# Down stages of a decoder layer: the last hidden pair is used later in the first product, and the row statistics of the later column groups are taken later in the next stage

## The chip, the cores and the metric

The kernel runs on one core of a Trainium2 chip. A core has five engines with instruction streams of their own: TensorE (PE in the profile; its weight loads, which overlap the products, are PEld), VectorE (DVE), ScalarE (ACT), GpSimd (POOL) and SyncE (SP), which here only starts transfers; 16 DMA engines carry them. The metric is the device time of one launch in microseconds (us).

## The reference

One inference step of one layer of a hybrid decoder, for a prompt of 1024 tokens and eight decode requests of one token each, 1032 rows in all. The model width is 1024, the hidden width of each feed-forward network (FFN) is 2816, and everything is float32.

```python
def swiglu(x, wg, wu, wd):
    return (jax.nn.silu(x @ wg) * (x @ wu)) @ wd

    h = x + 0.5 * swiglu(rmsnorm(x, lw['g_ff1']), lw['w_ff1_gate'], lw['w_ff1_up'], lw['w_ff1_down'])
    z = rmsnorm(h, lw['g_mix']) @ lw['w_in']
    ...
    mix = jnp.concatenate([rmsnorm(a, lw['g_attn_out']), hm], axis=-1) @ lw['w_out']
    h = h + mix
    h = h + 0.5 * swiglu(rmsnorm(h, lw['g_ff2']), lw['w_ff2_gate'], lw['w_ff2_up'], lw['w_ff2_down'])
    h = h + jax.nn.sigmoid(rmsnorm(h, lw['g_ple']) @ lw['w_ple_gate']) * (pe @ lw['w_ple_proj'])
```

Between `z` and `mix` stand attention with a low-rank latent cache (`a`) and an mLSTM with matrix memory (`hm`); a last `rmsnorm` follows. What matters here are the two FFNs, the product that stands behind each (`w_in` behind the first, `w_ple_gate` behind the second), and the row norm between them: `rmsnorm(h)` needs the sum of the squares of each row of `h` over all 1024 features.

## The kernel before

**Layout and arithmetic.** Activations lie with features on the 128 partitions and the 1032 tokens along the free axis, so `h` is eight tiles of 128 x 1032 (`KD` = 8, index k). For the projections the tokens are cut into three groups of 344 (`G`, index g), for the FFNs into four quarters of 258. A float32 product is made of three matmuls on rounded parts: high by high, high by low, low by high (`mm3`, L219 to L222). So each operand is first split: ScalarE writes the rounded high part, VectorE subtracts it from the original and writes the low part. Large tiles come from 43 shared SBUF buffers (`B`), short-lived ones of 344 columns from nine scratch buffers (`SC`), accumulators from eight PSUM banks (`PS`).

**An FFN** is one call of `ffn` (L425 to L697). Its first part makes the gate and up products and from them the hidden tiles, 22 of 128 features, in 11 pairs p (`NP`). It also forms the sums of tiles that the seven products of the next part need, and `store` (L461 to L470) writes them to a DRAM tensor `hidd[7, 2, 128, NP, QN]`: for each pair and each half hf of the columns two POOL transfers, `hid<-hp` (L469, products' operands 0 to 3) and `hid<-gs` (L470, operands 4 to 6). The last pair, 10, is stored last.

**The down stage** is a scheme of seven products i (table `DOWN`, L41 to L47) in place of eight. Each has two halves hf, each half walks the 11 pairs, and one step is one pair: twelve matmuls into four accumulators `pd`. That makes 7 x 2 x 11 = 154 steps (`NSTEP`). After the last pair of a half VectorE adds the four accumulators, times plus or minus one half, into two to four places of `h` (L677).

The loads that feed the steps are planned by step number. `at(n, fn)` puts a function on a heap, and `fetch(n)` runs all that are due before the matmuls of step n. `load_w` fetches a double pair of weights and plans its sum and its split 5, 6 and 7 steps later. `load_x` (L596 to L610) fetches the hidden tiles of four pairs from `hidd`, 11 steps before their first use (`X_LEAD`), and plans their high part on ScalarE (L603) 6 steps after the load and the low part on VectorE (L606) 7 steps after it. Its third load of a half holds pairs 8 to 10. `load_h` fetches the eight tiles of `h` from step -3 on, and `aheads` names steps at which weights of the next stage are loaded. Items with negative step numbers, and those up to step 4, are run inside the last chunk of the gate and up part.

All these loads are started by SyncE, which takes its instructions strictly in the written order; one that has to wait for a store blocks the ones behind it. Inside the down stage TensorE, SyncE, VectorE and ScalarE all keep the written order (`DOWN_ENGINES`, L657 to L684). Outside it TensorE and SyncE keep it, and a planner orders the other engines.

**The norm behind an FFN** is an object of class `Rows` (L307 to L337), `nu` before the input projection and `npl` before the last stage. `ops(g, k)` multiplies a tile of `h` by its gain and splits it into the operands of the next product (ScalarE L322, VectorE L323). `square(g, k)` squares it on ScalarE (L327) and adds it on VectorE (L331) to the running sum of the group, which takes a scratch buffer. `scale(g)` calls `norm_r` (L285): a matmul with a matrix of ones (`ns`, L287) sums over the partitions, ScalarE takes the reciprocal root (L291), and VectorE refines it with a Newton step. The result multiplies the product's output, not its input, so a product of group g needs `ops(g, k)` to start, and `scale(g)` before its evacuation; the code asserts that `scale(g)` is written before the unit.

Before the change the last ten steps of a down stage do `ops` of groups 0 and 1, two a step in the order of groups, one `square(0, k)` a step, and then `scale(0)`. `ops(2, k)` stands behind the last step. The sums of groups 1 and 2 belong to the generator `stats` (L686 to L697): for each of the two groups four ticks with two squares each, one empty tick, then `scale(g)`. The emitter (L115 to L152) advances a generator once per so many microseconds of *planned* time, which `em.spend` counts; for `stats` that is 1.2, and one unit of the following product spends 3.5.

**The stages behind.** The input projection (from L1158) runs 22 columns of weights times three groups, 66 units of 24 matmuls (`pz`, L220 to L222). `units(22, EARLY)` (L343) gives their order: the first `EARLY` columns go group by group, the rest column by column with the three groups in a row. So with `EARLY` = 3, group 1 starts at the fourth unit and group 2 at the seventh. `win_unit` (L851) loads weights three columns ahead. After unit (3, 0) the generator `gates` of the mLSTM's gates is started, one tick per 7 planned us; what is left of it is run at unit (9, 2). The last stage (`ple_unit`, L1733) runs eight columns times three groups, group by group, 24 units of 24 matmuls (`pl`); `final(g)` (L1769) is its norm.

Of the kernel before, what the change touches and what calls it, by code (L numbers as in the profile page):

```python
# [23 lines left out]
KD = D // 128  # L24
# [8 lines left out]
NWC = (NP + 1) // 2  # L33
NXC = (NP + 3) // 4
W_ISSUE = (-19, -15, -11, -8, -4, -1)
# [37 lines left out]
LAT_FIN = 12.0  # L73
EARLY = 3
LIFT_POOL = (0, 2, 4)
# [80 lines left out]
def trunk(ctx: ExitStack, tc, I, O):  # L156
# [267 lines left out]

    def ffn(build, X, pre, part, resid, h, nxt, ahead, aheads):  # L425

# [139 lines left out]
        def at(n, fn):  # L566
            heapq.heappush(items, (n, next(count), fn))
# [27 lines left out]

        def load_x(s, i, hf, t):  # L596
            n = min(4, NP - 4 * t)
            raws = [B([128, 4, QN], F32, "hr")]
            sp.dma_start(out=raws[0][:, 0:n], in_=hidd[DOWN[i][1][hf], hf, :, 4 * t:4 * t + n, :])

            def high():
                xh[i, hf, t] = [B([128, 4, QN], F32R, x) for x in ("hh", "hl")]
                act.copy(xh[i, hf, t][0][:, 0:n], raws[0][:, 0:n])  # L603

            def low():
                dve.tensor_tensor(out=xh[i, hf, t][1][:, 0:n], in0=raws[0][:, 0:n], in1=xh[i, hf, t][0][:, 0:n].bitcast(F32), op=ALU.subtract)  # L606
                raws.pop()

            at(s + X_HI, high)
            at(s + X_LO, low)  # L610

# [4 lines left out]
        for i in range(7):  # L616
# [4 lines left out]
            for hf in range(2):  # L621
                for t in range(NXC):
                    s = n + NP * hf + 4 * t - X_LEAD
                    at(s, lambda s=s, i=i, hf=hf, t=t: load_x(s, i, hf, t))
        for m in range(KD):
# [3 lines left out]
        n = NSTEP - NP + 1  # L629
        for g in range(2):  # L630
            for k in range(KD):
                at(n + (KD * g + k) // 2, lambda g=g, k=k: nxt.ops(g, k))
        for k in range(KD):
            at(n + k, lambda k=k: nxt.square(0, k))
        at(n + KD + 1, lambda: nxt.scale(0))

# [20 lines left out]
        ctx2 = ExitStack()  # L657
        ctx2.enter_context(tc.manual_schedule(engines={mybir.EngineType[x] for x in DOWN_ENGINES}))
        for n in range(NSTEP):
            fetch(n)  # L660
            i, hf, p = n // (2 * NP), n // NP % 2, n % NP
            if p == 0:
                acc = [PS([128, QN], "pd") for _ in range(4)]
            (whi, wlo), (xhi, xlo) = wdh[i, p // 2], xh[i, hf, p // 4]
            for m in range(4):
                c = slice(m * 128, (m + 1) * 128)
                mm3(acc[m], whi[:, p % 2, c], wlo[:, p % 2, c], xhi[:, p % 4, :], xlo[:, p % 4, :], p == 0, p == NP - 1)
            whi = wlo = xhi = xlo = None
            if hf == 1 and (p % 2 == 1 or p == NP - 1):
                wdh.pop((i, p // 2))  # L670
            if p % 4 == 3 or p == NP - 1:
                xh.pop((i, hf, p // 4))
            if p == NP - 1:
                for m in range(4):
                    for r, j, sign in DOWN[i][2]:
                        t = h[4 * r + m][:, QS[j if hf == 0 else 3 - j]]
                        dve.scalar_tensor_tensor(out=t, in0=acc[m], scalar=0.5 * sign, in1=t, op0=ALU.mult, op1=ALU.add)  # L677
                acc = None
            em.spend(1.44)
# [6 lines left out]
        def stats():  # L686
            for g in (1, 2):
                for k in range(KD):
                    nxt.square(g, k)
                    if k % 2:  # L690
                        yield
                yield
                nxt.scale(g)
# [120 lines left out]

    ffn(build1, X1, pre1, "1", lambda m: I["xT"][m * 128:(m + 1) * 128, :], h, nu, load_in, AH_IN)
    u = nu.x
# [337 lines left out]
    for n, (i, g) in enumerate(us):  # L1154
        win_unit(i, g)
        if (i, g) == (3, 0):
            em.add(gates_gen, 7.0)
# [570 lines left out]

    ffn(build2, X2, pre2, "2", lambda m: hsp2[m * 128:(m + 1) * 128, :], h, npl, load_p, AH_P)
    xp = npl.x  # L1730
# [174 lines left out]
```

## Time and profile before

| | |
|---|---|
| median of 3 runs | 2246.82 us (2246.46 to 2249.53) |
| the profiled execution's own time | 2244.91 us |
| span of its trace | 2243.1 us |
| busy: TensorE, VectorE, ScalarE, GpSimd | 96%, 65%, 41%, 14% |
| first down stage (first to last `pd`) | starts at 504.98 us |
| input projection | starts at 741.70 us |
| second down stage | starts at 1868.9 us |
| last stage | starts at 2108.8 us |

One execution is profiled; all times are in microseconds from the start of its span. Busy time of TensorE is the modelled time of pipelined matmuls, so 96% doesn't say that it runs at its best pace: at a lower granted clock the same matmul counts for longer. A row of waits names the waiting engine and line, then what it waited for, then the summed wait, how many there were, and the longest. A row of a window names its stretch and length, then for TensorE, its weight loads, VectorE, ScalarE and GpSimd the busy time with the number of instructions in brackets, then the granted clock (1.00 is full), the busy share of the DMA engines and GB/s. A row of the timeline has the start, the duration, the engine, the line and the operation, output before the arrow and inputs behind it.

### The profile page before, as it was taken

The numbers are of one execution on the slowest core, as the hardware profiler recorded it, in microseconds if no ns is written. First come the engines' busy times: TensorE is split into PE (matmuls) and PEld (weight loads), VectorE is DVE, ScalarE is ACT, GpSimd is POOL, SyncE is SP. The second block draws the span as 40 slices with busy tenths as digits, with TensorE's granted clock in tenths as the row PEclk, the third lists the DMA queues.
The fourth block names the chain that finished last, engine by engine and source line by source line (L and its number), as shares of the span: only waits on it lengthen the run. The fifth ranks groups of instructions, "written<-read, shape, count | busy, mean of one in ns | idle before, by whom it ended". The sixth has DMA issues, their size and how long they took to land.

```text
span 2243.1 us, 40124 instructions
## 1 busy us (share of the span) xinstructions
PE 2156.2 (96%) x16225; PEld 2045.1 (91%) x16225; DVE 1457.9 (65%) x2882; ACT 914.1 (41%) x1749; POOL 322.1 (14%) x353
## 2 busy tenths in 40 slices
PE   8999999998999999999999999999999998999787
PEld 7999999998999899999855579999999998999786
DVE  6756656566776647556666777775665655776846
ACT  6333333332343433434455653433333332333633
POOL 2000001000000021111277424100010100000012
PEclk8999999999999999999999999999999999999898
DMA  6122323239875422223555431232232337876213
GB/s 246 53 90 90 123 72 123 90 119 363 271 250 172 157 35 88 87 87 107 165 140 144 152 117 67 84 107 90 81 118 86 109 105 282 317 261 222 81 35 105
DMA packets 106242, 307.80 MB, mean 137 GB/s; under 512 B 14448, under 2 KB 32464, under 8 KB 106056
## 3 DMA queue, kind: packets, MB, share of 16 engines
q1 hardware_dynamic: 82200, 233.75, 31.3%
q0 software_dynamic: 20400, 67.26, 9.3%
q10 hardware_dynamic: 3456, 4.23, 0.7%
q8 instruction: 127, 2.08, 0.4%
q14 instruction: 59, 0.48, 0.1%
HBM read 236.61 MB, written 68.57 MB: 136 GB/s over the span
## 4 chain that ended last, share of the span: by engine, by line
PE 75%; issue 10%; DVE 8%; DMA 3%; ACT 2%; POOL 1%; SPq 0%; DVEq 0%; ACTq 0%; POOLq 0%
PE c L454 9%; PE c L455 9%; PE c L456 9%; PE pd L221 6%; PE pd L222 6%; PE pd L220 6%; PE pz L220 3%; PE pz L222 3%; PE pz L221 3%; PE pss L1482 3%; PE po L1537 2%; PE pT L1514 1%; PE pl L221 1%; PE pl L220 1%; PE pl L222 1%
## 5 line engine op out<-in xcount | busy, mean ns | idle before, releaser
L454 PE MATMUL c<-xh,wh 128*128 128x258 f32 x1920 | 543.3, 283 | 0.9 <-ACT u L532 0.9
L455 PE MATMUL c<-xl,wh 128*128 128x258 f32 x1920 | 542.5, 283 | 0.0
L456 PE MATMUL c<-xh,wl 128*128 128x258 f32 x1920 | 542.5, 283 | 0.0
L454 PEld LDWEIGHTS c<-xh,wh 128*128 128x128 f32 x1920 | 362.6, 189 | 1.5 <-ACT u L532 1.5
L455 PEld LDWEIGHTS c<-xl,wh 128*128 128x128 f32 x1920 | 363.7, 189 | 0.0
L456 PEld LDWEIGHTS c<-xh,wl 128*128 128x128 f32 x1920 | 362.6, 189 | 0.0
L221 PE MATMUL pd<-hl,wh 128*128 128x258 f32 x1232 | 352.0, 286 | 9.7 <-DVE hl L606 9.7
L220 PE MATMUL pd<-hh,wh 128*128 128x258 f32 x1232 | 351.8, 286 | 8.1 <-ACT hh L603 8.1
L222 PE MATMUL pd<-hh,wl 128*128 128x258 f32 x1232 | 350.8, 285 | 0.0
L206 DVE TENSOR_TENSOR wl<-wr,wh 128x1024 fp32r<-128x1024 f32 x166 | 207.4, 1250 | 72.5 <-ACT wh L202 39.4
L221 PEld LDWEIGHTS pd<-hl,wh 128*128 128x128 f32 x1232 | 236.0, 192 | 11.7 <-DVE hl L606 11.4
L220 PEld LDWEIGHTS pd<-hh,wh 128*128 128x128 f32 x1232 | 235.8, 191 | 9.5 <-ACT hh L603 9.1
L222 PEld LDWEIGHTS pd<-hh,wl 128*128 128x128 f32 x1232 | 235.9, 192 | 0.0
L202 ACT CAST wh<-wr 128x1024 fp32r<-128x1024 f32 x166 | 173.0, 1047 | 54.4 <-DVE wr L412 46.2
L585 ACT CAST wh<-wr 128x1024 fp32r<-128x1024 f32 x84 | 81.9, 977 | 253.9 <-issue 141.9
L220 PE MATMUL pz<-u,wh 128*128 128x344 f32 x528 | 172.9, 328 | 0.0
L222 PE MATMUL pz<-u,wl 128*128 128x344 f32 x528 | 169.1, 320 | 0.0
L221 PE MATMUL pz<-u,wh 128*128 128x344 f32 x528 | 168.9, 320 | 0.0
L470 POOL DMA_DIRECT2D hid<-gs x44 | 33.1, 751 | 838.8 <-DVE gs L465 700.5
L588 DVE TENSOR_TENSOR wl<-wr,wh 128x1024 fp32r<-128x1024 f32 x84 | 95.4, 1136 | 73.7 <-ACT wh L585 73.7
L606 DVE TENSOR_TENSOR hl<-hr,hh 128x1032 fp32r<-128x1032 f32 (+1 forms) x84 | 95.6, 1139 | 19.2 <-ACT hh L603 18.6
L220 PEld LDWEIGHTS pz<-u,wh 128*128 128x128 f32 x528 | 99.7, 189 | 0.7 <-issue 0.2
(406 smaller groups left out, 4592.5 us busy)
## 6 DMA issues: line engine op xcount, KB each, us to landing
wr<-in_wd SPq DMA_DIRECT2D x120, 512.0 KB, 5.1
hr<-hid SPq DMA_DIRECT2D x56, 516.0 KB, 5.1
hid<-hp POOLq DMA_DIRECT2D x44, 516.0 KB, 5.5
wr<-in_wg SPq DMA_DIRECT2D x44, 512.0 KB, 4.4
wr<-in_wu SPq DMA_DIRECT2D x44, 512.0 KB, 4.0
hid<-gs POOLq DMA_DIRECT2D x44, 387.0 KB, 4.3
wr<-in_w_in SPq DMA_DIRECT2D x22, 512.0 KB, 4.7
hr<-hid SPq DMA_DIRECT2D x28, 387.0 KB, 5.8
```

The costliest lines, as they stand in the source:

```text
L202: act.copy(hi, src)
L206: dve.tensor_tensor(out=lo, in0=src, in1=hi.bitcast(F32), op=ALU.subtract)
L220: pe.matmul(ps, whi, xhi, start=first, stop=False)
L221: pe.matmul(ps, whi, xlo, start=False, stop=False)
L222: pe.matmul(ps, wlo, xhi, start=False, stop=last)
L454: pe.matmul(ps, whi[:, c], xhi[:, k, :], start=first and k == 0, stop=False, skip_group_check=True)
L455: pe.matmul(ps, whi[:, c], xlo[:, k, :], start=False, stop=False, skip_group_check=True)
L456: pe.matmul(ps, wlo[:, c], xhi[:, k, :], start=False, stop=last and k == 3, skip_group_check=True)
L585: act.copy(wdh[i, c][0][:, 0:n], raws[0][:, 0:n])
L588: dve.tensor_tensor(out=wdh[i, c][1][:, 0:n], in0=raws[0][:, 0:n], in1=wdh[i, c][0][:, 0:n].bitcast(F32), op=ALU.subtract)
L606: dve.tensor_tensor(out=xh[i, hf, t][1][:, 0:n], in0=raws[0][:, 0:n], in1=xh[i, hf, t][0][:, 0:n].bitcast(F32), op=ALU.subtract)
L1482: pe.matmul(ps[:, 0:n], qp[:, qs], kp[0:96, kc], start=True, stop=True)
```

## The change

Six edits:

1. *Order of the first product.* A table `STEPS` gives the steps of each product. In the first product the step of half 0 and pair 10 moves behind the first four steps of half 1, from step 10 to step 14. Since half 0 is then unfinished while half 1 runs, each half has accumulators of its own (`accs`).
2. *Size of the loads.* A table `XC` gives the loads of hidden tiles. In the first product pairs 8 and 9 are one load and pair 10 is another, for both halves; the other six products keep pairs 8 to 10 together.
3. *Lead of the last load.* A load that holds pair 10 alone is planned 8 steps ahead of its use, with its two casts 4 and 5 steps later (`X_LATE`); the others keep 11, 6 and 7.
4. *Last ten steps of a down stage.* `ops(0, k)` go one a step, `square(0, k)` two a step, `ops(1, k)` start four steps later (one a step, then two), and `scale(0)` comes one step earlier.
5. *Statistics of groups 1 and 2.* `ffn` takes a parameter `lag`, the number of empty ticks between the last square of a group and its `scale`: 5 for the first FFN, 14 for the second, in place of 1. For the first FFN `EARLY` goes from 3 to 4, so that group 1 starts at the fifth unit and group 2 at the ninth.
6. *Gates.* The generator `gates` is started after unit (4, 0), not (3, 0).

```diff
-NXC = (NP + 3) // 4
+
+STEPS = [[(hf, p) for hf in range(2) for p in range(NP)] for _ in range(7)]
+STEPS[0] = STEPS[0][0:10] + STEPS[0][11:15] + [(0, 10)] + STEPS[0][15:]
+XC = [((0, 4), (4, 4), (8, 2), (10, 1))] + [((0, 4), (4, 4), (8, 3))] * 6
+X_LATE = (8, 4, 5)
...
-EARLY = 3
+EARLY = 4
...
-        def load_x(s, i, hf, t):
-            n = min(4, NP - 4 * t)
+        def load_x(s, i, hf, t, s_hi, s_lo):
+            p0, n = XC[i][t]
             raws = [B([128, 4, QN], F32, "hr")]
-            sp.dma_start(out=raws[0][:, 0:n], in_=hidd[DOWN[i][1][hf], hf, :, 4 * t:4 * t + n, :])
+            sp.dma_start(out=raws[0][:, 0:n], in_=hidd[DOWN[i][1][hf], hf, :, p0:p0 + n, :])
...
-            at(s + X_HI, high)
-            at(s + X_LO, low)
+            at(s + s_hi, high)
+            at(s + s_lo, low)
...
-                for t in range(NXC):
-                    s = n + NP * hf + 4 * t - X_LEAD
-                    at(s, lambda s=s, i=i, hf=hf, t=t: load_x(s, i, hf, t))
+                for t, (p0, _) in enumerate(XC[i]):
+                    lead = X_LATE if p0 == NP - 1 else (X_LEAD, X_HI, X_LO)
+                    s = n + STEPS[i].index((hf, p0)) - lead[0]
+                    at(s, lambda s=s, i=i, hf=hf, t=t, lead=lead: load_x(s, i, hf, t, *lead[1:]))
...
-        for g in range(2):
-            for k in range(KD):
-                at(n + (KD * g + k) // 2, lambda g=g, k=k: nxt.ops(g, k))
         for k in range(KD):
-            at(n + k, lambda k=k: nxt.square(0, k))
-        at(n + KD + 1, lambda: nxt.scale(0))
+            at(n + k, lambda k=k: nxt.ops(0, k))
+            at(n + 4 + min(k, 4 + (k - 4) // 2), lambda k=k: nxt.ops(1, k))
+            at(n + k // 2, lambda k=k: nxt.square(0, k))
+        at(n + KD, lambda: nxt.scale(0))
...
+        accs = [None, None]
         for n in range(NSTEP):
             fetch(n)
-            i, hf, p = n // (2 * NP), n // NP % 2, n % NP
+            i = n // (2 * NP)
+            hf, p = STEPS[i][n % (2 * NP)]
             if p == 0:
-                acc = [PS([128, QN], "pd") for _ in range(4)]
+                accs[hf] = [PS([128, QN], "pd") for _ in range(4)]
+            acc = accs[hf]
...
-                yield
+                for _ in range(lag):
+                    yield
                 nxt.scale(g)
                 yield
...
-        if (i, g) == (3, 0):
+        if (i, g) == (4, 0):
             em.add(gates_gen, 7.0)
```

The calls of `ffn` pass `lag` as 5 and 14.

More of the change, by code (lines that the diff above doesn't have):

```diff
@@ L423, in weights, with ffn @@
         return work
-    def ffn(build, X, pre, part, resid, h, nxt, ahead, aheads):
+    def ffn(build, X, pre, part, resid, h, nxt, ahead, aheads, lag):
         W = [I["wg" + part], I["wu" + part]]
@@ L658, in ffn @@
         ctx2.enter_context(tc.manual_schedule(engines={mybir.EngineType[x] for x in DOWN_ENGINES}))
+        accs = [None, None]
         for n in range(NSTEP):
             fetch(n)
-            i, hf, p = n // (2 * NP), n // NP % 2, n % NP
+            i = n // (2 * NP)
+            hf, p = STEPS[i][n % (2 * NP)]
             if p == 0:
-                acc = [PS([128, QN], "pd") for _ in range(4)]
-            (whi, wlo), (xhi, xlo) = wdh[i, p // 2], xh[i, hf, p // 4]
+                accs[hf] = [PS([128, QN], "pd") for _ in range(4)]
+            acc = accs[hf]
+            t = next(t for t, (p0, k) in enumerate(XC[i]) if p0 <= p < p0 + k)
+            x = p - XC[i][t][0]
+            last = x == XC[i][t][1] - 1
+            (whi, wlo), (xhi, xlo) = wdh[i, p // 2], xh[i, hf, t]
             for m in range(4):
                 c = slice(m * 128, (m + 1) * 128)
-                mm3(acc[m], whi[:, p % 2, c], wlo[:, p % 2, c], xhi[:, p % 4, :], xlo[:, p % 4, :], p == 0, p == NP - 1)
+                mm3(acc[m], whi[:, p % 2, c], wlo[:, p % 2, c], xhi[:, x, :], xlo[:, x, :], p == 0, p == NP - 1)
             whi = wlo = xhi = xlo = None
@@ L670, in ffn @@
                 wdh.pop((i, p // 2))
-            if p % 4 == 3 or p == NP - 1:
-                xh.pop((i, hf, p // 4))
+            if last:
+                xh.pop((i, hf, t))
             if p == NP - 1:
@@ L677, in ffn @@
                         dve.scalar_tensor_tensor(out=t, in0=acc[m], scalar=0.5 * sign, in1=t, op0=ALU.mult, op1=ALU.add)
-                acc = None
+                acc = accs[hf] = None
             em.spend(1.44)
@@ L813, in load_in @@
         win_w[i] = loadw(I["w_in"][i], KD)
-    ffn(build1, X1, pre1, "1", lambda m: I["xT"][m * 128:(m + 1) * 128, :], h, nu, load_in, AH_IN)
+    ffn(build1, X1, pre1, "1", lambda m: I["xT"][m * 128:(m + 1) * 128, :], h, nu, load_in, AH_IN, 5)
     u = nu.x
@@ L1727, in load_p @@
         wp[j] = loadw(I["w_pg"][j], KD)
-    ffn(build2, X2, pre2, "2", lambda m: hsp2[m * 128:(m + 1) * 128, :], h, npl, load_p, AH_P)
+    ffn(build2, X2, pre2, "2", lambda m: hsp2[m * 128:(m + 1) * 128, :], h, npl, load_p, AH_P, 14)
     xp = npl.x
```

## The prediction

> **What bounds the kernel now.** First the page's head, the engines' shares and the chain that ended last.
>
> ```profile
> span 2243.1 us, 40124 instructions
> PE 75%; issue 10%; DVE 8%; DMA 3%; ACT 2%; POOL 1%; SPq 0%; DVEq 0%; ACTq 0%; POOLq 0%
> ```
>
> TensorE carries three quarters of the chain, so time is to be had only where it stands still or runs slowly. The second view, TensorE's own waits, says where.
>
> ```profile
> PE ns L287 <- DVE sq L331: 25.2, 5, 10.9
> PE pd L221 <- DVE hl L606: 9.7, 8, 3.4
> PE pd L220 <- ACT hh L603: 8.1, 5, 2.4
> ```
>
> The longest are exactly the two that the change touches: the row statistic (`ns`) waiting for the sum of squares, and the down stage (`pd`) waiting for its split operands. The third view, windows of the trace, prices them with all their consequences; "x" counts matmuls, and the granted clock and the share of the DMA engines stand behind the engines.
>
> ```profile
> 496.00:508.00 12.00, 12.00 (x103) 12.00 (x102) 9.27 (x21) 4.55 (x6) 0.88 (x2) 1.00 0.02 6
> 505.00:556.00 51.00, 41.44 (x319) 40.01 (x318) 30.45 (x46) 10.77 (x12) 3.00 (x4) 0.93 0.96 363
> 556.00:736.00 180.00, 180.00 (x1504) 180.00 (x1503) 133.83 (x187) 73.19 (x92) 0.00 (x0) 1.00 0.69 226
> 736.00:742.00 6.00, 4.78 (x36) 4.37 (x35) 4.47 (x9) 3.66 (x7) 0.00 (x0) 1.00 0.69 228
> 749.00:764.00 15.00, 10.84 (x56) 9.88 (x55) 11.58 (x23) 4.32 (x10) 0.00 (x0) 0.89 0.75 262
> 764.00:804.00 40.00, 40.00 (x256) 40.00 (x255) 13.52 (x33) 6.86 (x10) 5.84 (x11) 1.00 0.29 42
> 1869.00:1920.00 51.00, 42.73 (x314) 41.49 (x313) 30.39 (x46) 10.89 (x12) 3.04 (x4) 0.90 0.96 364
> 2100.00:2109.00 9.00, 6.66 (x40) 5.98 (x40) 6.74 (x14) 4.81 (x9) 0.00 (x0) 0.81 0.51 155
> 2116.00:2155.00 39.00, 21.53 (x104) 20.01 (x103) 22.45 (x40) 20.78 (x37) 3.07 (x3) 0.74 0.07 18
> 2155.00:2177.00 22.00, 22.00 (x142) 22.00 (x141) 9.41 (x18) 7.55 (x15) 3.75 (x5) 1.00 0.17 49
> ```
>
> Undisturbed, the down stage does 1504/180 = 8.36 matmuls a microsecond, the input projection 256/40 = 6.40, the last stage 142/22 = 6.45. At these paces the first entry into a down stage lost 51 − 319/8.36 = 12.8 us, the second 51 − 314/8.36 = 13.4. Around the statistics, the first FFN lost 6 − 36/8.36 = 1.7 and 15 − 56/6.40 = 6.2; the second 9 − 40/8.36 = 4.2 and 39 − 104/6.45 = 22.9. Together **26.2 at the entries and 35.0 at the statistics**: 61.2 us of idle and half-clock time, the most that the change could return there.
>
> **What makes the entries slow.** SyncE's waits, its queue, the store for which it waits (from the chain), and the loads behind it:
>
> ```profile
> SPq L599 <- DMA hid<-hp: 41.8, 2, 20.9
> 512.13 0.33 SPq L599 DMA_DIRECT2D hr<-hid  x1
> 512.56 1.24 SPq L614 DMA_DIRECT2D h<-in_xT  x2
> 507.86 4.20 DMA hid<-hp
> h<-in_xT SPq DMA_DIRECT2D x8, 516.0 KB, 9.5
> 514.00:556.00 42.00, 32.70 (x248) 31.48 (x247) 23.20 (x32) 10.77 (x12) 0.00 (x0) 0.92 1.02 396
> ```
>
> The third load of hidden tiles holds pairs 8 to 10. Pair 10 is stored last (issued 507.86, landed 4.20 later), so SyncE stands 20.9 us, from 491.2 to 512.1, once per FFN, and behind it queue eight rows of `h`, weights and the other half's tiles. The DMA engines idle (0.02 of 496 to 508) and then are full at 396 GB/s for 42 us. Loads land late; TensorE starves.
>
> **The change, part by part.** *Entry.* Pairs 8 and 9 get a load of their own, pair 10 another, eight steps ahead of a product moved from step 10 to step 14 of the first stage. The 8–9 load needs a store issued a whole chunk earlier, so SyncE passes it near 492 and feeds the queue behind it through the idle time. 20.9 us × 396 GB/s is 8.3 MB; the eight rows of `h` are 8 × 516 KB, 4.2 MB, so the backlog should be gone before step 4 instead of 556. This holds only if the waits follow the exact pieces stored, not the span they enclose. The stores bear on that:
>
> ```profile
> L470 POOL DMA_DIRECT2D hid<-gs x2: 744/744/744, 506.6 to 508.6; - x2
> L469 POOL DMA_DIRECT2D hid<-hp x2: 757/766/774, 507.9 to 509.3; - x2
> DMA to landing us min/median/max: 3.4/4.9/6.7
> ```
>
> The two halves' stores interleave in memory, and yet the second pair was issued at 508.6 and 509.3, before the first could have landed (506.6 + 3.4 = 510.0). So pieces seem to be told apart. Bounds: gain 0 to 26.2. I take 25.0: the 0.6 left at each entry is the step 4 to 6 loss, where VectorE is busy with the last stores' sums.
>
> The late pair: a step is 12/8.36 = 1.44 us; step 6 comes at 505 + 8.6 = 513.6, its use at step 14 at 525.1. SyncE may stand until 512.1 to 516 for the store, the load lands some 5 us later, the casts take under 2: ready by 523. Behind it on SyncE queue the next stage's weights, behind its cast on ScalarE and VectorE those weights' casts, due at step 22. Each FFN gains two DMAs, two casts and two subtractions:
>
> ```profile
> L603 ACT CAST hh<-hr x84: 823/1051/1061, 498.3 to 2091.9; 128x1032 fp32r<-128x1032 f32 x56, 128x774 fp32r<-128x774 f32 x28
> L606 DVE TENSOR_TENSOR hl<-hr,hh x84: 957/1225/1234, 500.2 to 2097.5; 128x1032 fp32r<-128x1032 f32 x56, 128x774 fp32r<-128x774 f32 x28
> ```
>
> By the two sizes, 0.88 and 1.04 ns a column, a split load costs a fixed 0.14 us more on ScalarE and 0.15 on VectorE; 134 of 180 us busy on VectorE hides it. The eight accumulators of the first stage fill eight PSUM banks only from step 10 to 14, while the next four are wanted at step 22.
>
> *Group 0's statistic.* Squares go in two a step, `scale` one step earlier, the copies of group 1 spread to the last step; no instruction more. The sum is ready some three steps before it is read, so the 1.2 and 2.3 us waits (in the 1.7 and 4.2 above) go. VectorE, full in these steps, finishes group 1's copies and group 2's up to 2 us later against TensorE; the eight PSUM banks cover that.
>
> *Groups 1 and 2.* The statistics generator ticks every 1.2 planned us and a unit spends 3.5. Now `scale(1)` comes at the 6th tick, after two units; `scale(2)` at the 12th, after four. With lag 5 they fall after units 4 and 7 of the input projection (10th and 20th tick), with lag 14 after 7 and 13 of the last stage (19th and 38th). When are the sums ready?
>
> ```profile
> 2118.50 2.37 ACT L327 ACTIVATE sq<-h 128x344 f32<-128x344 f32 x6
> 2125.59 1.85 DVE L331 TENSOR_TENSOR sq<-sq,sq 128x344 f32<-128x344 f32 x2
> 2127.49 1.52 PE L287 MATMUL ns<-sq,ones 128*128 128x344 f32 x2 [10.94 <-DVE sq L331]
> L220 PE MATMUL pl<-xp,wh x192: 313/320/995, 2108.8 to 2224.9; 128*128 128x344 f32 x192
> 741.70 0.32 PE L220 MATMUL pz<-u,wh 128*128 128x344 f32 x1
> 750.92 1.22 DVE L206 TENSOR_TENSOR wl<-wr,wh 128x1024 fp32r<-128x1024 f32 x1
> 752.48 1.06 DVE L331 TENSOR_TENSOR sq<-sq,sq 128x344 f32<-128x344 f32 x2
> 761.00 0.51 DVE L331 TENSOR_TENSOR sq<-sq,sq 128x344 f32<-128x344 f32 x1
> ```
>
> In the last stage (from 2108.8) the sum was ready 18.6 us in; a unit is 24/6.45 = 3.72 us, so seven units are 26.0: 7 us to spare. In the input projection (from 741.7) it was ready 11.8 and 19.8 us in, wanted at 15.0 and 26.3. What is late next is there the fourth weight column, which four units of a group need at 3 × 3.75 = 11.3 us; its low half was done 10.4 us in. The rows of `h` keep their 8 of 43 buffers two units longer and each sum one of nine scratch buffers for five to nine more: hidden, since no weight load is planned before unit 12, and by the slack of the PSUM banks. Bounds: 20 us (VectorE becomes the limit, below) to 35.0. I take 32: one us for that column, two for VectorE in the last stage.
>
> *Gates* start after unit 12 instead of 9 and end with a forced finish at the same unit 29; nine ticks of seven us fit where eleven were.
>
> ```profile
> md<-g POOLq DMA_DIRECT2D x2, 0.1 KB, 8.3
> ```
>
> Its slowest hop is that one; the last two pieces now come together. Cost 0 to 8.3; I take 0.5, since the hop with 8.3 comes at the third tick, far from the end.
>
> **Sum.** 25.0 + 32.0 − 0.5 = 56.5. The profiled execution took 2244.9 (1.8 more than its span); the median 2246.8 lies 1.9 above it. 2246.8 − 56.5 = **2190**.
>
> **A rule against it.** The store's 4.20 us above was measured while the loads' queue was quiet; with loads running it was up to 6.7. By the Trainium skill (DMA: Bandwidth & Descriptors, Queues, rings and completion order) each DMA engine alternates between the queues' rings packet by packet, so loads fed early share with the stores. The trace agrees as far as 4.20 against 6.7 go; that is the second rival's mechanism.
>
> **Rivals.** *The 8–9 load still waits for the last store*: the change wouldn't do what it says, and the entries stay: 2246.8 − 31.5 = 2215. For it: nothing in the trace has read a neighbouring piece just after a store. Against: the stores above. 0.10.
>
> *The late pair is late.* Twice the quiet landing for the store, and a load with eight 1.3-us transfers (512 KB at 396 GB/s) ahead of it, 10.4 us: 507.9 + 8.4 + 10.4 + 2 = 528.7, 3.6 us past 525.1; and half a dip of the clock (0.92 over 42 us is 6.7 us at half) costs 1.7: some 5.3 per FFN, 10.6 in all: 2201 (up to 2206). Against: by then the rows of `h` are through. 0.10.
>
> *VectorE bounds the last stage.* Its groups from 2109 to 2128:
>
> ```profile
> L206 DVE TENSOR_TENSOR wl<-wr,wh 128x1024 fp32r<-128x1024 f32 x4 | 4.9, 1220 | 0.0
> L331 DVE TENSOR_TENSOR sq<-sq,sq 128x344 f32<-128x344 f32 x7 | 4.3, 616 | 1.7 <-ACT sq L327 1.4
> L323 DVE SCALAR_TENSOR_TENSOR xp<-h,gc,xp 128x344 fp32r<-128x344 f32 x8 | 4.0, 572 | 0.0
> L677 DVE SCALAR_TENSOR_TENSOR h<-pd,h 128x258 f32<-128x258 f32 x4 | 1.4, 418 | 0.0
> ```
>
> These 14.6 us, a Newton step (4 operations) and 24 products of the same 128x344, half a microsecond each (14), make 28.6, against 8 × 3.72 = 29.8 of TensorE. With 0.6 us of hand-over a unit (an estimate: one such operation) it ends 3.6 us behind, and a dip of the clock adds 2 to 4: 2196 to 2198, up to 2205 at the bound above. 0.11.
>
> *Slower*: the last stage at half clock. If VectorE's hand-over stops TensorE a little in every unit, the 22 units after the second run at the pace seen after the long wait:
>
> ```profile
> 2128.50:2131.90 3.40, 3.40 (x12) 3.16 (x12) 2.05 (x5) 1.92 (x3) 0.00 (x0) 0.50 0.16 52
> ```
>
> 12 matmuls in 3.4 us, 6.8 us a unit: 22 × 3.1 = 68 us lost, 12 more than is won: 2258. It decides once each few units hold an idle stretch long enough to lower the clock; 2155 to 2177 ran at 1.00 with VectorE at 43%. 0.03. The Trainium skill (TensorE: Matmul & The Clock Gate, Part 1: The HAM clock gate) has the clock halved after an idle window of about 3.4 us; the 0.50 behind the 10.94 us wait agrees.
>
> **How the numbers follow.** Forecast 0.62 (own range 2185 to 2197: from all 61 us to 50), rivals 0.10, 0.10, 0.11, 0.03; 0.04 is left for orders of VectorE's and ScalarE's work that come out worse elsewhere. 2182 to 2212 leaves out the first rival, the slower one and that rest, 0.17. About 0.2% is what a measurement can tell here. Faster: 0.62 + 0.10 + 0.10 + 0.11 = 0.93; of the rest 0.02 same, 0.05 slower.
>
> **What would show it.** SyncE issuing the third `hr` near 492 and no row `hid<-hp` of 20 us; the DMA engines busy from 496 to 508; about 425 matmuls in the first 51 us of each down stage; no `ns <- sq` above 1 us; the last stage at clock 1.00 with some 3.75 us a unit. The forecast is wrong if `pd` still waits over 3 us per entry, if a new wait on `hl` stands at step 14, or if `pl` waits for `wl`.

## The result and the profile after

The changed kernel takes 2194.36 us (median of 4 runs, 2193.0 to 2196.5) against 2246.64: a ratio of 0.977, 95% interval 0.975 to 0.978, so 52.3 us less; forecast were 56.5 less, 2190. Line numbers are now 4 higher at `pd` and 11 higher at `pl`. First the page's head, the chain that ended last, and TensorE's waits:

```profile
span 2192.4 us, 40143 instructions
PE 80%; issue 7%; DVE 7%; ACT 3%; DMA 2%; POOL 1%; ACTq 0%; DVEq 0%; SPq 0%; POOLq 0%
```

```profile
PE ns L1783 <- POOL sq L1771: 6.5, 1, 6.5
...
PE pd L225 <- DVE hl L610: 2.2, 2, 1.1
...
PE pd L224 <- ACT hh L607: 1.0, 2, 0.5
```

No `ns` waits for a sum of `Rows` any more, and `pd` waits for 3.2 us in all, 17.8 before. New at the top is the last norm: `ns` at L1783 waits 6.5 us for GpSimd's sum, 3.2 before (behind the last `pl`). The windows that answer to those of before:

```profile
499.00:507.50 8.50, 8.50 (x74) 8.50 (x73) 6.40 (x12) 6.45 (x9) 0.00 (x0) 1.00 0.98 377
507.50:558.50 51.00, 49.40 (x408) 48.83 (x407) 36.80 (x55) 13.88 (x17) 2.99 (x4) 1.00 0.95 361
...
739.00:754.00 15.00, 15.00 (x96) 14.80 (x95) 12.35 (x23) 5.05 (x11) 0.00 (x0) 1.00 0.83 317
1853.30:1904.30 51.00, 49.44 (x409) 48.99 (x408) 36.88 (x55) 13.68 (x16) 2.99 (x4) 1.00 0.95 360
...
2084.60:2123.60 39.00, 39.00 (x248) 38.78 (x247) 28.39 (x51) 22.16 (x43) 7.12 (x6) 1.00 0.13 37
```

The DMA engines are full before the first `pd` (0.98, where it was 0.02). The first 51 us of the down stages hold 408 and 409 matmuls, 319 and 314 before: (89 + 95)/8.36 = **22.0 us won at the entries**, some 2 us lost in each still (a second profile of the same kernel, `changed, again` below, has 415 and 411: 23.1 us). Around the statistics TensorE stands nowhere and the clock is 1.00. By the first and the last product of each stage, in us; the experiments below explain the other names:

| kernel | first down stage | input projection | second down stage | last stage | last product to end |
|---|---|---|---|---|---|
| before | 236.7 | 295.0 | 239.7 | 116.7 | 17.6 |
| changed | 224.4 | 289.2 | 224.3 | 94.2 | 20.6 |
| changed, again | 223.5 | 289.1 | 224.1 | 94.1 | 20.7 |
| entry_only | 225.9 | 297.8 | 226.4 | 117.1 | 17.4 |
| stats_only | 235.2 | 289.4 | 234.5 | 94.3 | 20.8 |
| split_no_move | 227.1 | 289.3 | 229.9 | 94.2 | 20.6 |
| move_no_split | 236.1 | 289.1 | 234.7 | 94.3 | 20.8 |
| old_tail | 227.4 | 289.4 | 227.3 | 95.3 | 17.4 |
| lag_1_1 | 223.6 | 296.3 | 223.7 | 117.6 | 17.4 |
| fetch0 | 224.6 | 289.1 | 223.8 | 94.2 | 20.6 |
| step18 | 222.4 | 289.7 | 223.2 | 94.2 | 20.6 |
| pool_adds | 226.0 | 289.0 | 224.4 | 94.3 | 23.4 |
| no_root | 225.7 | 289.1 | 223.5 | 94.1 | 19.5 |
| s18_lag13 | 222.8 | 289.4 | 222.8 | 94.3 | 17.1 |

From before to changed: 12.3 + 5.8 + 15.4 + 22.5 - 3.0 = 53.0 us; the profiled execution shows 50.7, because its start (to the first `pd`) happened to take 2.5 us longer, which the second profile of the same kernel doesn't show (505.1 again). Of the rows, `changed`, `changed, again`, `lag_1_1`, `fetch0`, `pool_adds` and `no_root` have in effect the same plan of loads and products at both ends of the first down stage, and they spread from 223.5 to 226.0 us. In `pool_adds` and `no_root`, the two longest, 3.4 us at half the clock stand behind the two short waits that are left at the entry; at half clock that costs 1.7 us. So a microsecond or two in one row proves nothing by itself.

Why something is left at the entries: SyncE's wait, its queue, and what POOL, VectorE and ScalarE did meanwhile (waits, then timelines):

```profile
SPq L603 <- DMA hid<-hp: 29.7, 2, 14.9
```

```profile
494.70 0.33 SPq L603 DMA_DIRECT2D hr<-hid  x1
506.22 0.33 SPq L618 DMA_DIRECT2D h<-in_xT  x1
521.42 0.33 SPq L603 DMA_DIRECT2D hr<-hid  x1
505.49 1.22 DVE L592 TENSOR_TENSOR wl<-wr,wh 128x1024 fp32r<-128x1024 f32 x1
507.63 1.23 DVE L610 TENSOR_TENSOR hl<-hr,hh 128x1032 fp32r<-128x1032 f32 x1
509.71 1.22 DVE L592 TENSOR_TENSOR wl<-wr,wh 128x1024 fp32r<-128x1024 f32 x1
510.85 0.69 DVE L610 TENSOR_TENSOR hl<-hr,hh 128x516 fp32r<-128x516 f32 x1
514.09 0.76 DVE L471 TENSOR_TENSOR hp<-hp 128x258 f32<-128x258 f32 x2
514.88 1.50 POOL L473 DMA_DIRECT2D hid<-hp  x2
524.43 0.41 ACT L607 CAST hh<-hr 128x258 fp32r<-128x258 f32 x1 [4.61 <-DMA hr<-hid]
524.88 0.43 DVE L610 TENSOR_TENSOR hl<-hr,hh 128x258 fp32r<-128x258 f32 x1 [1.56 <-ACT hh L607]
```

The load of pairs 8 and 9, half 0's third, goes at 494.70, and the eight rows of `h` pass by 506.6. SyncE still stands 14.9 us per FFN, now at pair 10's load: from 506.6 to 521.4. What it waits for is the first of the two stores in the row `hid<-hp`: the trace has it wait for that store's semaphore. This store goes at 514.9, 7.4 us into the stage, 2.9 before (507.86 and 504.98), and it takes 6.5 us until SyncE is free, 4.2 before. It goes late because VectorE has the early loads' casts, four in the rows above (1.22 + 1.23 + 1.22 + 0.69 us), ahead of the last pair's sums. Pair 10 is split by 525.3, and step 14 is at 507.5 + 14 x 1.435 = 527.6: in time. Meanwhile the DMA engines fall to 0.36 (a window), and what stands behind pair 10 is loaded late. VectorE's timeline ahead of the remaining wait, and the groups of ScalarE and of TensorE, by shape, at it:

```profile
521.00:525.00 4.00, 4.00 (x36) 4.00 (x35) 1.36 (x2) 0.41 (x1) 0.00 (x0) 1.00 0.36 65
...
531.55 2.75 DVE L687 SCALAR_TENSOR_TENSOR h<-pd,h 128x258 f32<-128x258 f32 x8
534.82 1.22 DVE L584 TENSOR_TENSOR wr<-wr,wr 128x1024 f32<-128x1024 f32 x1
538.34 1.56 DVE L610 TENSOR_TENSOR hl<-hr,hh 128x1032 fp32r<-128x1032 f32 x2
...
L607 ACT CAST hh<-hr 128x258 fp32r<-128x258 f32 x1 | 0.4, 398 | 0.0
...
L224 PE MATMUL pd<-hh,wh 128*128 128x258 f32 x1 | 0.4, 387 | 0.5 <-ACT hh L607 0.5
L225 PE MATMUL pd<-hl,wh 128*128 128x258 f32 x1 | 0.4, 386 | 1.1 <-DVE hl L610 1.1
```

TensorE waits from 538.0 on, for a cast of 258 columns: that is the single load of *half 1's* pair 10, used in step 21. (The expectations below speak of step 22, as I first read it.) On ScalarE and VectorE its casts stand behind the next product's first weights and hidden tiles, which are not due before step 22. Two things make these late, and both come from the change. Their weights were loaded late, because SyncE stood: VectorE waits 2.76 us for the first of them, until 528.07. And the eight additions into `h` that end half 0 now fall into this stretch, since half 0 ends four steps later: the second weights had landed by 531.5, but VectorE, which does the additions first, begins their sum (L584) at 534.82, with no idle time before it. The additions take 2.75 us, more than the two waits together (0.5 + 1.1 us).

### The profile page after: what moved, and what is told of

Read it like the earlier page. It is cut to its first block, busy times and chain, and to the rows that moved or that the text cites. A ratio compares the mean times of both kernels' runs of the same rounds, so it can differ in the third digit from the quotient of the medians.

```text
span 2192.4 us, 40143 instructions
## 1 busy us (share of the span) xinstructions
PE 2138.2 (98%) x16225; PEld 2032.4 (93%) x16225; DVE 1458.2 (67%) x2886; ACT 913.0 (42%) x1753; POOL 324.0 (15%) x353
## 4 chain that ended last, share of the span: by engine, by line
PE 80%; issue 7%; DVE 7%; ACT 3%; DMA 2%; POOL 1%; ACTq 0%; DVEq 0%; SPq 0%; POOLq 0%
PE c L458 10%; PE c L460 10%; PE c L459 10%; PE pd L225 7%; PE pd L226 7%; PE pd L224 7%; PE pz L224 4%; PE pz L225 4%; PE pz L226 4%; PE pss L1493 2%; PE po L1548 1%; PE pT L1525 1%; PE cp L459 1%; PE cp L460 1%; PE cp L458 1%
## 5 line engine op out<-in xcount | busy, mean ns | idle before, releaser
L592 DVE TENSOR_TENSOR wl<-wr,wh 128x1024 fp32r<-128x1024 f32 x84 | 95.3, 1135 | 69.0 <-ACT wh L589 69.0
L610 DVE TENSOR_TENSOR hl<-hr,hh 128x1032 fp32r<-128x1032 f32 (+3 forms) x88 | 96.0, 1093 | 9.0 <-ACT hh L607 4.9
L518 ACT COPY c<-c 128x258 f32<-128x258 f32 x80 | 30.1, 376 | 171.0 <-PE c L460 171.0
```

The source lines that it names most:

```text
L592: dve.tensor_tensor(out=wdh[i, c][1][:, 0:n], in0=raws[0][:, 0:n], in1=wdh[i, c][0][:, 0:n].bitcast(F32), op=ALU.subtract)
```

## Experiments

### The two halves

`entry_only` undoes the edits behind the down stages, `stats_only` those at the entry.

```diff
 entry_only: ops, square and scale of the last ten steps as before
-EARLY = 4
+EARLY = 3
-                for _ in range(lag):
-                    yield
+                yield
-        if (i, g) == (4, 0):
+        if (i, g) == (3, 0):
```

> Only the edits at the entry of the down stages (order of the first product, split load, late lead); the last ten steps, the lag, the order of the input projection and the start of the gates as before. Theory: the two halves of the change touch different idle times and add up. In the changed kernel the first 51 us of the two down stages hold 408 and 409 matmuls against 319 and 314 before, (89 + 95)/8.36 = 22 us; so 2246.6 - 22 = 2225 us (2221 to 2229), with the long waits of ns back. Rival: part of the entries' gain is only there because the rest of the change shifts the stages, or the statistics' waits grow when the stage before is faster: above 2230 or below 2219.

```diff
 stats_only
-STEPS[0] = STEPS[0][0:10] + STEPS[0][11:15] + [(0, 10)] + STEPS[0][15:]
-XC = [((0, 4), (4, 4), (8, 2), (10, 1))] + [((0, 4), (4, 4), (8, 3))] * 6
+XC = [((0, 4), (4, 4), (8, 3))] * 7
```

> Only the edits behind the down stages (order of the last ten steps, lag 5 and 14, four early columns, gates after unit (4, 0)); loads and the order of the first product as before. Theory: all of the 35.0 us lost around the statistics return, and some 3 us go into the end of the last stage, where VectorE is behind: 2246.6 - 32 = 2215 us (2211 to 2219), together with the other half 52 to 54. Rival: the halves do not add up (the sum of the two gains is under 48 or over 58).

Measured: 2228.0 us, ratio 0.991 (0.990 to 0.993), and 2213.8, ratio 0.985 (0.984 to 0.987), beside 2247.84 of before: 19.8 and 34.0 us, together 53.8. The halves add up, as expected. By the table each moves its own stages, with one exception: in `entry_only` the input projection is 2.8 us longer than before (27.0 us of waits for sums instead of 25.2 in all, and 6.8 us at half clock in the projection instead of 3.4). That the statistics' waits grow when the stage before is faster, which the expectation named as a rival, is so to that extent. The waits stay where the half is missing; of `entry_only`, then of `stats_only`:

```profile
PE ns L291 <- DVE sq L335: 27.0, 6, 11.8
```

```profile
PE pd L224 <- DVE hl L609: 9.3, 8, 3.4
```

### The entry: split, move, or both

```diff
 split_no_move
-STEPS[0] = STEPS[0][0:10] + STEPS[0][11:15] + [(0, 10)] + STEPS[0][15:]
```

> The changed kernel, but pair 10 of half 0 stays at step 10; its load is still its own, 8 steps ahead. Theory: in the changed kernel this load starts at 521.4, as soon as the last store has landed, and is split by 525.3; step 10 comes at 507.5 + 10 x 1.435 = 521.9, so TensorE stands 3 to 4 us in each entry and runs some us at half clock behind it: 2194.4 + 7 to 12, 2201 to 2207 us. Rival: the move buys nothing, the split alone frees the queue: 2192 to 2196.

```diff
 move_no_split
-XC = [((0, 4), (4, 4), (8, 2), (10, 1))] + [((0, 4), (4, 4), (8, 3))] * 6
+XC = [((0, 4), (4, 4), (8, 3))] * 7
```

> The changed kernel, but pairs 8 to 10 of the first product are one load again, planned 11 steps ahead of step 8; pair 10 of half 0 is still used at step 14. Theory (the blocked queue is what cost the entries): SyncE stands from about 492 to the last store's landing, step 8 starves and everything behind is late; the entries lose 12 to 14 us each again: 2194.4 + 20 to 26, 2214 to 2221 us, with SyncE's wait for the store back at 20 us. Rival (the late pair itself was what cost): 2194 to 2203.

Measured: 2200.0 us (ratio 0.979, 0.977 to 0.981) and 2217.0 (0.987, 0.985 to 0.989). So the split frees the queue, and the move without it is worth nothing: `stats_only`, which has neither, took 2213.8 us on the same chip, 3.2 less. SyncE stands for the store as before. Its waits and its queue in `move_no_split`:

```profile
SPq L603 <- DMA hid<-hp: 40.9, 2, 20.5
```

```profile
491.28 0.33 SPq L603 DMA_DIRECT2D hr<-hid  x1
513.67 0.33 SPq L603 DMA_DIRECT2D hr<-hid  x1
```

`split_no_move` lost 2.7 and 5.6 us in its two down stages, a little less than expected, and not where expected. Its waits, and ScalarE's and VectorE's timelines:

```profile
PE pd L224 <- DVE hl L609: 5.8, 2, 3.4
...
SPq L602 <- DMA hid<-hp: 34.9, 2, 18.4
...
520.88 0.41 ACT L606 CAST hh<-hr 128x258 fp32r<-128x258 f32 x1 [12.49 <-DMA hr<-hid]
528.55 1.05 ACT L606 CAST hh<-hr 128x1032 fp32r<-128x1032 f32 x1 [1.23 <-DMA hr<-hid]
528.50 2.75 DVE L686 SCALAR_TENSOR_TENSOR h<-pd,h 128x258 f32<-128x258 f32 x8
531.17 1.22 DVE L609 TENSOR_TENSOR hl<-hr,hh 128x1032 fp32r<-128x1032 f32 x1
```

Pair 10 of half 0 was there for step 10 (507.3 + 14.4 = 521.7; split from 520.9 on): SyncE stood for its store at an earlier place, and it was fed as soon as the store had landed. Late was half 1's load of pairs 4 to 7, behind it in SyncE's order, cast at 528.6 for step 15 (507.3 + 21.5 = 528.8); and its low half stands on VectorE behind the eight additions into `h` that end half 0, which the move puts four steps later. So by this trace the move is worth its 5.6 us by what it does for the second half, not for pair 10: with the move, the load of pair 10 is planned two steps behind that of half 1's pairs 4 to 7, not two steps ahead of it.

Two tries to remove the rest:

```diff
 fetch0
-                    fetch(-8 * (6 - ("b11", "b21", "t2", "t1", "t3", "t4", "b22").index(n)) + 4)
+                    fetch(-8 * (6 - ("b11", "b21", "t2", "t1", "t3", "t4", "b22").index(n)))
```

> The changed kernel, but the loads and casts planned for steps 1 to 4 are written behind the end of the gate and up part, not inside it. Theory: what still waits at step 22 of each down stage (0.5 + 1.1 us) waits because SyncE stands some 15 us at the load of pair 10, and the last stores come late (513 to 516 us) because VectorE does casts for steps 1 to 4 (1.2 + 0.7 us) ahead of their sums; with these behind the sums the stores go some 2 us earlier, SyncE stands some 13 us, and the waits at step 22 go or shrink to half: 2191 to 2193.5 us. Rival: VectorE is full there, and the two orders cost the same, or casts come late: 2194 to 2198.

```diff
 step18
-STEPS[0] = STEPS[0][0:10] + STEPS[0][11:15] + [(0, 10)] + STEPS[0][15:]
+STEPS[0] = STEPS[0][0:10] + STEPS[0][11:19] + [(0, 10)] + STEPS[0][19:]
```

> The changed kernel with pair 10 of half 0 at step 18 instead of 14, so that its load is planned at step 10 (507.5 + 14.4 = 521.9), when the last store has landed. Theory: SyncE's wait for the store goes to under 2 us, the loads behind it are fed 14 us earlier, and the waits at step 22 (1.6 us per entry and some time at half clock) go: 2190 to 2193 us. Rival: the waits at step 22 come from the DMA engines, which are full there, and stay: 2193 to 2196.

These two, `old_tail` and `pool_adds` ran on another chip, on which the attention part between the two stages takes some 900 us instead of 832 (before: 2319.3 us there). So their stages in the table count, and the ratios.

`fetch0`: ratio 0.978 (0.976 to 0.981), stages as in the changed kernel. VectorE still did the same four casts ahead of the sums, the stores went no earlier, and SyncE stood 15.2 us. The edit did not change what it was to change: that the casts delay the stores is read from the order, not tried.

`step18`: ratio 0.976 (0.974 to 0.978), an interval that overlaps with that of `fetch0`, so the gain is read from the stages. Its down stages are 2.0 and 1.1 us shorter than in the changed kernel's profile, and shorter than in any of the six profiles named under the table; `s18_lag13` below has them at 222.8 and 222.8. The waits at pair 10 of half 1 are gone in the first, and 0.6 us is left in the second:

```profile
PE pd L225 <- DVE hl L610: 0.6, 1, 0.6
...
SPq L603 <- DMA hid<-hp: 26.4, 2, 13.4
...
506.90:557.90 51.00, 51.00 (x426) 50.90 (x425) 39.08 (x62) 14.04 (x17) 3.00 (x4) 1.00 0.96 365
1917.00:1968.00 51.00, 50.41 (x421) 50.19 (x420) 38.33 (x60) 13.85 (x17) 3.00 (x4) 1.00 0.96 363
```

426 matmuls in 51 us are 8.35 a microsecond, the undisturbed pace. But SyncE did not stop standing: still 13.4 us, against under 2 expected. SyncE is not tied to TensorE's steps: what waits for nothing it issues at once, so it reached the load planned for step 10 at 510.3, 11 us before that step. Two things are better here, and the run does not separate them. More loads stand ahead of the one that waits: half 1's pairs 8 and 9 and the next product's first weights are issued by 510.0, not at 521.8 to 524.1. And the eight additions into `h` now stand behind the casts of half 1's pair 10 (534.36 behind 532.88), not ahead of them.

### The statistics: order, lag

```diff
 old_tail
+        for g in range(2):
+            for k in range(KD):
+                at(n + (KD * g + k) // 2, lambda g=g, k=k: nxt.ops(g, k))
         for k in range(KD):
-            at(n + k, lambda k=k: nxt.ops(0, k))
-            at(n + 4 + min(k, 4 + (k - 4) // 2), lambda k=k: nxt.ops(1, k))
-            at(n + k // 2, lambda k=k: nxt.square(0, k))
-        at(n + KD, lambda: nxt.scale(0))
+            at(n + k, lambda k=k: nxt.square(0, k))
+        at(n + KD + 1, lambda: nxt.scale(0))
```

> The changed kernel with the last ten steps of both down stages ordered as before (copies of groups 0 and 1 two a step, one square of group 0 a step, scale(0) a step later). Theory: this order carries group 0's statistic alone; the waits of 1.2 and 2.3 us for its sum come back with their half-clock time, which before cost 1.7 and 4.2 us: 2194.4 + 5.9 = 2200 us (2198 to 2203). Rival: the lag and the four early columns carry everything: 2193 to 2196.

```diff
 lag_1_1
-    ffn(build1, ..., h, nu, load_in, AH_IN, 5)
-    ffn(build2, ..., h, npl, load_p, AH_P, 14)
+    ffn(build1, ..., h, nu, load_in, AH_IN, 1)
+    ffn(build2, ..., h, npl, load_p, AH_P, 1)
```

> The changed kernel with lag 1 behind both FFNs, as before; the order of the last ten steps, the four early columns and the gates stay changed. Theory: the lag carries the gain of groups 1 and 2, since their sums are ready no earlier than before: one wait of 4 to 5 us in the input projection (its cost before 6.2 us) and two, of 11 and 6.5 us, in the last stage (22.9 us), while the end of the last stage gets 3 us shorter again: 28 - 3 = 25 to 29 us longer than the changed kernel. Rival: copies and squares in the new order make the sums ready in time, or the planner moves the squares up: under 15 us longer.

`old_tail`: ratio 0.979 (0.976 to 0.981). Both down stages are 3.0 us longer and the two waits for group 0's sum are back (3.5 us together), so the new order carries that statistic. Not all of the 3.0 in the first stage is its cost: at the entry the clock was 0.97 (396 matmuls in the first 51 us instead of 408), which is 1.4 us. With the 1.1 us more in the last stage the old order costs 1.6 + 3.0 + 1.1 = 5.7 us, against 5.9 counted. But the end is 17.4 us, 3.2 shorter, so the whole loses less than expected.

`lag_1_1`: 2222.0 us, ratio 0.990 (0.988 to 0.991), beside 2193.4 of the changed kernel on the same chip: 28.7 longer, at the upper end of what was expected. The lag carries the gain of groups 1 and 2. Waits of `old_tail`, then of `lag_1_1`:

```profile
PE ns L291 <- DVE sq L335: 3.5, 2, 2.3
```

```profile
PE ns L291 <- DVE sq L335: 23.7, 3, 12.4
```

### The end of the last stage

In `lag_1_1`, `entry_only` and `old_tail` the end is 17.4 us, in the changed kernel 20.6. What makes it longer? The changed kernel run again, as the measure:

> The changed kernel itself, as the measure for the three others on one chip. The ratio to the kernel before should be the first one's, 0.975 to 0.978; its last stage should again end some 20.6 us behind its last product (17.6 before), by every theory.

2193.4 us, ratio 0.977 (0.975 to 0.978); the end 20.7.

```diff
 pool_adds
-                dve.tensor_tensor(out=self.acc[g], in0=self.acc[g], in1=q, op=ALU.add)
+                eng = pool if self.g0 == G_PLE and g else dve
+                eng.tensor_tensor(out=self.acc[g], in0=self.acc[g], in1=q, op=ALU.add)
```

> The changed kernel with the 14 sums of squares of groups 1 and 2 behind the second FFN on GpSimd instead of VectorE. Theory: the last stage ends 3 us later behind its last product than before (wait of ns for GpSimd's sum 6.5 instead of 3.2 us) because VectorE is behind TensorE through the stage; 14 x 0.52 = 7.3 us less on VectorE let it catch up, and the wait goes back to about 3.2: 2191 us (2190 to 2192.5). Rival: the end is set by the norm of group 1 (five products of 0.9 us on VectorE) that falls among the last units wherever VectorE stands, or GpSimd slows VectorE: 2193.5 to 2197.

Ratio 0.979 (0.976 to 0.981), and the end is 23.4 us, longer, not shorter. This does not decide whether VectorE's load matters, because the edit put new waits in the place of the work. A sum takes 1.04 us on GpSimd and 0.56 on VectorE; VectorE stood 4.3 us for GpSimd's sums and 4.2 us for casts of weights, where it stood for neither in the changed kernel, and that is more than the 7.3 us of work taken away. VectorE is the slower engine there: in the last stage of the changed kernel it never waits for a product `pl`, and before it did so for 18.7 us. VectorE's group that waits for the sigmoid, and ScalarE's timeline around the first root of the changed kernel, show where it stands instead:

```profile
L1764 DVE TENSOR_TENSOR sg<-sg,pj 128x344 f32<-128x344 f32 x24 | 15.3, 639 | 18.8 <-ACT sg L1761 18.8
...
2099.73 1.28 ACT L295 ACT_TABLE_LOAD   x1
2104.79 0.55 ACT L295 ACTIVATE rr<-ns,epsc 128x344 f32<-128x344 f32 x1 [3.77 <-PE ns L291]
...
2106.35 1.28 ACT L1761 ACT_TABLE_LOAD   x1
2107.64 0.49 ACT L1761 ACTIVATE sg<-sg 128x344 f32<-128x344 f32 x1
2108.17 0.52 DVE L1764 TENSOR_TENSOR sg<-sg,pj 128x344 f32<-128x344 f32 x1 [5.77 <-ACT sg L1761]
```

The planner has put group 1's root behind the fourth sigmoid on ScalarE, but TensorE makes the `ns` for it only after the seventh unit. ScalarE changes its table, waits 3.77 us, and changes back; VectorE, in its fixed order, stands 5.77 us. In all it stands 18.8 us for sigmoids, 13.9 before. Two kernels on this; `no_root` leaves out two of the reciprocal roots:

```diff
 no_root (root of groups 1 and 2 behind the second FFN)
-        act.activation(r, ps, RSQ, bias=epsc, scale=1.0 / d)
+        act.activation(r, ps, AF.Copy, scale=1.0 / d)
```

> The changed kernel with the reciprocal root of groups 1 and 2 behind the second FFN (ScalarE) replaced by a scaled copy, so that the last norm's input is not the reference's there; place and number of instructions stay, but ScalarE needs no change of its function table there, which costs 1.28 us each way. Theory: the end of the last stage is 3 us later than before because ScalarE's changes of table between sigmoids hold up VectorE, which waits for each sigmoid, and not because VectorE has too much to do; four loads of 1.28 us less give 2 to 4 us back, 17 to 18.5 us from the last product to the end. Rival: VectorE's place among the last units is set by its own work: the time stays within 1 us of the changed kernel's.

```diff
 s18_lag13: step18, and
-    ffn(build2, ..., h, npl, load_p, AH_P, 14)
+    ffn(build2, ..., h, npl, load_p, AH_P, 13)
```

> The changed kernel with pair 10 at step 18 and lag 13 behind the second FFN. By the traces, step 18 took 2.0 and 1.1 us out of the two down stages. With lag 13 the roots of group 2 and of the last norm's group 0 stand side by side on ScalarE and share one change of table (two loads of 1.28 us less), and scale(1) comes one unit earlier, 1.9 us behind its sum. Theory: 3 us from step 18 and 1 to 3 us at the end: 4 to 6 us faster than the changed kernel. Rival: the sum is late for lag 13, TensorE waits and runs at half clock: no faster than the changed kernel.

`no_root`: 2190.4 us, ratio 0.976 (0.974 to 0.977), intervals that overlap with the changed kernel's; the end 19.5 us, 1.2 shorter. Neither the 2 to 4 expected nor nothing. ScalarE's timeline says why, and the group under it what is left:

```profile
2104.27 0.46 ACT L298 ACTIVATE rr<-ns 128x344 f32<-128x344 f32 x1 [5.06 <-PE ns L291]
2128.57 0.46 ACT L298 ACTIVATE rr<-ns 128x344 f32<-128x344 f32 x1 [2.58 <-PE ns L291]
...
L1767 DVE TENSOR_TENSOR sg<-sg,pj 128x344 f32<-128x344 f32 x24 | 15.9, 662 | 17.0 <-ACT sg L1764 17.0
```

Without the loads ScalarE comes to the root sooner and waits longer for `ns`: 5.06 instead of 3.77, and 2.58 where it had not waited. So by this trace the place of the root against TensorE's `ns` counts as well as the table.

`s18_lag13`: 2187.1 us, ratio 0.974 (0.972 to 0.975), 6.3 us below the changed kernel on the same chip; the end is 17.1. This is the fastest kernel of the study.

```profile
2098.28 0.55 ACT L295 ACTIVATE rr<-ns,epsc 128x344 f32<-128x344 f32 x1
...
2126.45 0.55 ACT L295 ACTIVATE rr<-ns,epsc 128x344 f32<-128x344 f32 x1 [0.57 <-PE ns L291]
2127.28 0.54 ACT L1786 ACTIVATE r<-ns,epsc 128x344 f32<-128x344 f32 x1
...
L1764 DVE TENSOR_TENSOR sg<-sg,pj 128x344 f32<-128x344 f32 x24 | 14.7, 611 | 13.1 <-ACT sg L1761 13.1
```

The first root now finds `ns` done, the second waits 0.57, and it stands beside the last norm's, with one table for both. VectorE stands 13.1 us, 5.7 less: its wait at the first root falls from 5.77 to 2.68 us, the one at the second from 2.55 to 0.59. Step 18 is not what shortens the end, since `step18` alone ends at 20.6. `old_tail` agrees: with the lag of 14 its first root also finds `ns` done and its second also stands beside the last norm's, VectorE stands 14.1 us, and the end is 17.4. In both runs the wait and the shared table changed together, so how much each gives at the end is not told apart. Over the runs the end follows VectorE's standing for sigmoids: 13.1 to 14.1 us go with ends of 17.1 to 17.6 (before, `entry_only`, `old_tail`, `lag_1_1`, `s18_lag13`), 17.0 with 19.5, and 18.3 and 18.8 with 20.6 (`step18`, changed); `pool_adds`, with 18.0 and its other waits, ends at 23.4.

The Trainium skill (ScalarE: Activation LUTs, Table sets: the hidden batching unit) has calls batched by table set, which the shared load agrees with. The Trainium skill (ScalarE: Activation LUTs, What ACT_TABLE_LOAD costs) gives about 2.66 us for a change, 1.28 of load and some 1.38 of drain; here the load takes 1.28 us, but the function starts 1.29 us after its load began (2106.35 to 2107.64), so this trace shows no such drain.

## Why the prediction was right, step by step

*The forecast.* 2190 with 2182 to 2212; measured 2194.4. The likeliest case is the one that came: the rivals with the 8-9 load waiting, the late pair late at its own step, and the last stage at half clock did not; the one with VectorE behind in the last stage came in part.

*Entry, 25.0 forecast, 22.0 measured.* The mechanism held: the 8-9 load went at 494.7 (forecast near 492), without waiting for the last store, the DMA engines were full before the stage, and `split_no_move` and `move_no_split` show the split to be the part that frees the queue. The step that failed is "SyncE may stand until 512.1 to 516 for the store": it stood until 521.4, 13.9 us into the stage where 7 to 11 were forecast. The store was issued 4.5 us later in the stage than before and landed 2.3 us more slowly. I had taken its time of issue from before, when VectorE did the last pair's sums ahead of the casts; fed early, it does casts first. That the pair itself was ready 17.8 us into the stage, as forecast (18.0), is luck: the store was late, but the load landed in 3.0 us, with the DMA engines at 0.36, not in 5. But what I named behind it, the next product's weights and their casts, I priced at nothing, since they are due at step 22 only; I had overlooked that half 1's own pair 10 has its casts behind them and is due at step 21, and that the move puts eight additions of VectorE just ahead of them. That is the 1.6 us wait that `step18` takes out, and with it, in some executions, 3.4 us at half clock. The 0.6 that I left per entry, at steps 4 to 6, was not there: those waits are gone.

The rule held against the change says that loads share the DMA engines with the stores (the Trainium skill, DMA: Bandwidth & Descriptors, Queues, rings and completion order); the store for which SyncE waits took 6.5 us here (issued at 514.9, SyncE free at 521.4) with the DMA engines at 0.93 to 1.03 from 507.5 to 521, and 4.2 before. So the trace agrees, and pair 10 was in time all the same.

*Group 0's statistic.* Both waits are gone; `old_tail` brings them back. Right, and 5.7 us, as counted (1.7 + 4.2); the 6.0 us that the two down stages show in the table hold 1.4 us of clock at the entry, which are not the statistic's.

*Groups 1 and 2, 32 forecast for all the statistics.* The 35.0 us of waiting and half clock are gone to within a microsecond, and 3.0 came back at the end: 32.0. That this agrees to the tenth is luck, since the parts differ from what I took. In the input projection the gain is 5.8 of 6.2, so the fourth weight column and the gates together cost some 0.4, where I had allowed 1 and 0.5. The two us that I allowed for VectorE in the last stage came as 3.0, but for another reason than I gave. I had it bounded by VectorE's work alone, 28.6 against 29.8 us. VectorE is the slower engine there, but what my sum left out is that it stands for ScalarE: 18.8 us for sigmoids against 13.9 before, most of the difference behind a root that was planned too early against `ns`. Where that root does not wait and the second shares a table (`old_tail`, `s18_lag13`), VectorE catches up and the 3 us are gone. The rival "VectorE bounds the last stage" gave 3.6 us behind and a dip of the clock: the lateness came, the dip didn't (TensorE has no wait in that stage, and its clock is 1.00).

*The sum.* 22.0 + 32.0 = 54.0 by the windows against 56.5, and 52.3 by the medians; of the 4.2 us missing to the forecast, 3.0 are the entries' term; the rest no run assigns.

## What to carry to other kernels

When an engine that issues loads in order waits for a store, give the late piece a load of its own and put it as far back in the order as its use allows: that SyncE still stands 13 to 15 us costs little once nothing that is due soon stands behind it. Before moving work away from the engine that looks late, read what ends its idle time: here VectorE stood for sigmoids, and what went with the cure was the place of two roots in ScalarE's order, against the product that feeds one and beside a root with the same table for the other. Price what is queued behind each new wait, and look again at who is fed early: work that can start sooner may be done ahead of the work that you count on.

## What was not expected of the hardware

Two waits of TensorE of 0.5 and 1.1 us, one matmul apart, sometimes cost half the clock and sometimes nothing. The profiles of kernels with the changed entry hold eight entries with this pair of waits. In five the granted clock stayed at 1.00, the changed kernel's two among them; in three (`old_tail`, `pool_adds`, `no_root`) 3.4 us at 0.50 stand right behind the pair. In the other eight entries, with the wait of about 1.1 us alone or with one of 0.2 us, the clock stayed at 1.00. Behind the pair in `no_root`:

```profile
537.90:541.31 3.41, 3.41 (x18) 3.41 (x17) 2.46 (x5) 1.87 (x2) 0.00 (x0) 0.50 1.04 410
```

What decides between the two is not shown. Before the change, with waits of up to 3.4 us, the clock was 0.93 over the first 51 us. And nearly the same program took some 70 us more in its attention part on one chip than on another, while the stages compared here agree between chips to about a microsecond; `fetch0`, whose stages are the changed kernel's, had a ratio of 0.978 there.
